# A hybrid encoder block on one core: the score matmul over the low rotary keys with 128 rows in place of 64

## The chip, the core and the metric

The kernel runs on one core of a Trainium2 chip. A core has five engines that run their own instruction streams and meet through semaphores: PE (the matrix engine, with its weight loads shown as PEld), DVE (vector), ACT (scalar), POOL and SP, which here only starts transfers. The metric is the device time of one execution in microseconds (us), as the median of several runs. Times inside an execution come from one execution that the hardware profiler recorded.

## What is computed

One layer of an encoder block is applied to two batches of 512 tokens, each of width 1024, in float32. The input is normalised and projected; a convolution branch and an attention branch follow, are gated, summed and projected again. The change lies in the attention branch, cut here to what matters:

```python
q = rms_norm(q, q_head_g)            # 8 heads, 128 plain + 64 rotary columns
k = rms_norm(k, k_head_g)            # the 64 rotary columns are shared by the heads
q = concat([q[..., :128], apply_rope(q[..., 128:], cos, sin)])
k = concat([k[..., :128], apply_rope(k[..., 128:], cos, sin)])
s = einsum('bqhd,bkhd->bhqk', q, k) / sqrt(192)
o = einsum('bhqk,bkhd->bqhd', softmax(s), v)
```

## The kernel before

PE works on operands in a 32-bit form of reduced precision (float32r). To keep the accuracy, each float32 operand is split into a high part, rounded to that form, and a low part, the difference; a product is the sum of high by high, high by low and low by high. So one logical matmul is several instructions that accumulate in one PSUM bank.

The program has stages: the input projection and the convolution branch (to about 640 us), the latent projections (to about 740 us), the attention (to about 1030 us), and two dense blocks, the output projection of the attention (L228) and the last projection (L864). The stage of interest is the attention. It runs over 16 units, a unit being one head and one batch, and in each unit over four blocks of 128 queries, so there are 64 blocks.

`stage_a` (L524 on) prepares a unit in four pieces, run one unit ahead: keys and values (L540 to L542, banks pkv), queries (L568 to L570, bank pq), and the transposed operands of the scores. The rotary keys are scaled on POOL (`krs`, L561). The tile `kk` holds them in three slots of 64 columns: slots 0 and 1 get the rounded high part twice from ACT (L562), slot 2 gets the low part from POOL (L563), which subtracts the high part from `krs`. PE transposes the two high slots together (L600, four instructions of 128 by 128) and the low slot (L602, four of 128 rows by 64 columns); ACT copies the results to SBUF as `k1` (L604, 128 rows: the high part twice, one under the other) and `k2` (L605, 64 rows: the low part). The rotary queries `qrT` hold the high part in rows 0 to 63 and the low part in rows 64 to 127.

`scores` (L608 on) makes one block: five matmuls of 512 columns into one bank `sc`, L612 to L614 for the 128 plain dimensions, L615 with all 128 rows of `qrT` against `k1` (high by high plus low by high in one instruction), and L616 with rows 0 to 63 of `qrT` against `k2` (high by low). Then DVE takes the row maximum (L619, L620), ACT the exponential with its sum (L622), DVE divides (L623, L624). Two blocks later `transp` (L631) transposes the probabilities on PE, ACT and DVE split them (L632, L633), and `av` (L641 to L643) multiplies by the values.

The order in which the engines get their instructions is not written out by hand in this stage: the code is a loop over blocks, and a scheduler in the tile framework, which runs the program on its own timing model, places the instructions of each engine. A change in an instruction's size can therefore move others. In each engine's queue instructions run in that order. All tiles of eight PSUM banks come from one pool (`bank`).

Of the kernel before, what the change touches and what calls it, by code (L numbers as in the profile page):

```python
# [10 lines left out]
F32R = mybir.dt.float32r  # L11
# [6 lines left out]
P = 128  # L18
D = 1024
S = 512  # L20
# [3 lines left out]
RD = 64  # L24
# [19 lines left out]
def encoder_block(tc, xp_d, xs_d, win_d, wkr_d, whd_d, wqr_d, wo_d, wp_d, wout_d, vec_d, dwk_d, rg_d, rc_d, yp_d, ys_d):  # L44
    nc = tc.nc
    opened = {}

    def open_pool(name, **kw):
        if kw.get("space") is not DRAM:
            kw["reuse_waits"] = "tile"  # L50
        cm = tc.tile_pool(name=name, **kw)
        opened[name] = cm
        return cm.__enter__()
# [5 lines left out]
    f = lambda ap: ap.bitcast(F32)  # L59
    mm = nc.tensor.matmul  # L60
# [7 lines left out]
    def bc(ap, n):  # L68
        return ap.unsqueeze(2).to_broadcast([ap.shape[0], ap.shape[1], n])
# [17 lines left out]
    identr = cp.tile([P, P], F32R, name="identr")  # L87
# [89 lines left out]
    def rsqrt(out, v):  # L177
        nc.gpsimd.tensor_tensor(out, v, mhalf[:, : v.shape[1]], op=ALU.pow)
# [57 lines left out]
    def block(i, xh=hh, xl=hl, ahead=2):  # L236
        ps = fresh(i)
        block_mm(ps, i, xh, xl, (0, 1))
        prep(i + ahead)
        return flat(ps)  # L240
# [77 lines left out]
    for j in range(KD):  # L318
        ps = flat(first[0]) if j == 0 else block(J["cb", j])
# [3 lines left out]
        ps = flat(first[1]) if j == 0 else block(J["ca", j])  # L323
        u = cv.tile([P, 2, UW], F32, tag="u", name=f"u{j}", bufs=4)
# [82 lines left out]
    for j in range(KD):  # L407
        ps = block(J["p", j], lambda k, b: cH[k][:, b * S : (b + 1) * S], lambda k, b: cL[k][:, b * S : (b + 1) * S])
# [8 lines left out]
    tx = open_pool("tx", bufs=2, side="left")  # L417
# [3 lines left out]
    def tmp(shape, name):  # L421
        return tx.tile(shape, F32, tag="tmp", name=name, bufs=4)
# [60 lines left out]
    qrT = {}  # L483
# [40 lines left out]
    def stage_a(h, b):  # L524
        whi, wlo = wdone[J["h", h]]
        qh_w, ql_w = (w[:, : 3 * P].rearrange("p (k c) -> p k c", k=3) for w in (whi, wlo))
        kh_w, kl_w = (w[:, 3 * P : 896].rearrange("p (k c) -> p k c", k=2) for w in (whi, wlo))
        u = f"{h}_{b}"
        s4 = slice(4 * b, 4 * b + 4)
        r = {}  # L530
        two = lambda tag, shape=None, bufs=2: at.tile(shape or [P, S], F32R, tag=tag, name=f"{tag}{u}", bufs=bufs)

        pk = two_banks(f"pkv{u}", F32)
        for i, ps in enumerate(pk):
            for t2 in range(2):
                o = (2 * i + t2) * P
                for k in range(2):
                    kh_ = lat["kv", 0, k, b][:, o : o + P]
                    kl_ = lat["kv", 1, k, b][:, o : o + P]
                    mm(ps[:, t2], kh_, kh_w[:, k], start=(k == 0), stop=False)  # L540
                    mm(ps[:, t2], kh_, kl_w[:, k], start=False, stop=False)  # L541
                    mm(ps[:, t2], kl_, kh_w[:, k], start=False, stop=(k == 1))  # L542
        ksq_ = tmp([P, 4, P], f"ksq{u}")
        sk = tx.tile([P, 4], F32, tag="sk", name=f"sk{u}")
        rk = tx.tile([P, 4], F32, tag="rk", name=f"rk{u}")
        for i in range(2):
            ACT(ksq_[:, 2 * i : 2 * i + 2], pk[i][:, :, 0:P], AF.Square)
        DVE.reduce_sum(sk, ksq_, axis=AX.X)
        DVE.tensor_add(sk, sk, skr[:, s4])
        DVE.tensor_scalar(sk, sk, 1.0 / QKD, EPS, op0=ALU.mult, op1=ALU.add)  # L550
        rsqrt(rk, sk)
        vh, vl = two("vh", [P, 4, P], bufs=3), two("vl", [P, 4, P], bufs=3)
        for i in range(2):
            sl = slice(2 * i, 2 * i + 2)
            nc.scalar.copy(vh[:, sl], pk[i][:, :, P : 2 * P])
            DVE.tensor_sub(vl[:, sl], pk[i][:, :, P : 2 * P], f(vh[:, sl]))
        r["vh"], r["vl"] = vh, vl
        yield r
        krs = tx.tile([P, 4, RD], F32, tag="krs", name=f"krs{u}", bufs=1)
        kk = tx.tile([P, 4, 3, RD], F32R, tag="big", name=f"kk{u}")  # L560
        nc.gpsimd.tensor_mul(krs, kro[:, s4], bc(rk, RD))  # L561
        nc.scalar.copy(kk[:, :, 0:2], krs.unsqueeze(2).to_broadcast([P, 4, 2, RD]))  # L562
        nc.gpsimd.tensor_sub(kk[:, :, 2], krs, f(kk[:, :, 0]))  # L563

        ps = bank([P, S], F32, f"pq{u}")
        for k in range(3):
            xh_, xl_ = lat["cq", 0, k, b], lat["cq", 1, k, b]
            mm(ps, qh_w[:, k], xh_, start=(k == 0), stop=False)  # L568
            mm(ps, qh_w[:, k], xl_, start=False, stop=False)
            mm(ps, ql_w[:, k], xh_, start=False, stop=(k == 2))  # L570
        sqt = tmp([P, S], f"qsq{u}")
        ACT(sqt, ps, AF.Square)
        r["qh"], r["ql"] = two("qh"), two("ql")
        ACT(r["qh"], ps, AF.Identity, scale=gqk)
        DVE.scalar_tensor_tensor(r["ql"], ps, gqk, f(r["qh"]), op0=ALU.mult, op1=ALU.subtract)
        ks = tmp([P, 4, P], f"ks{u}")
        for t in range(4):
            ACT(ks[:, t], pk[t // 2][:, t % 2, 0:P], AF.Identity, scale=rk[:, t : t + 1])
        yield r
        pst = bank([P, 4], F32, f"pqs{u}")  # L580
        for t in range(4):
            mm(pst[:, t : t + 1], sqt[:, t * P : (t + 1) * P], ones[:, 0:1], start=True, stop=True)  # L582
        sv = tx.tile([P, 4], F32, tag="sv", name=f"sv{u}")
        DVE.tensor_add(sv, pst, ssr[:, s4, h])
        DVE.tensor_mul(sv, sv, rq2[:, s4])
        DVE.tensor_scalar_add(sv, sv, QKD * EPS)
        rsqrt(sv, sv)
        r["sq"] = sqs[h, b]
        DVE.tensor_mul(r["sq"], sv, rq[:, s4])

        pT = bank([P, S], F32, f"pkT{u}")
        for t in range(4):
            nc.tensor.transpose(pT[:, t * P : (t + 1) * P], ks[:, t], identf)
        r["kh"], r["kl"] = two("kh"), two("kl")
        nc.scalar.copy(r["kh"], pT)
        DVE.tensor_sub(r["kl"], pT, f(r["kh"]))
        pT1 = bank([P, S], F32R, f"pkr1{u}")
        pT2 = bank([RD, S], F32R, f"pkr2{u}")
        for t in range(4):
            nc.tensor.transpose(pT1[:, t * P : (t + 1) * P], kk[:, t, 0:2].rearrange("p a d -> p (a d)"), identr)  # L600
        for t in range(4):
            nc.tensor.transpose(pT2[:, t * P : (t + 1) * P], kk[:, t, 2], identr)  # L602
        r["k1"], r["k2"] = two("k1"), two("k2", [RD, S])
        nc.scalar.copy(r["k1"], f(pT1))  # L604
        nc.scalar.copy(r["k2"], f(pT2))  # L605
        yield r

    def scores(h, b, j, r):  # L608
        u = f"{h}_{b}_{j}"
        js = slice(j * P, (j + 1) * P)  # L610
        ps = bank([P, S], F32, f"sc{u}")
        mm(ps, r["qh"][:, js], r["kh"], start=True, stop=False)  # L612
        mm(ps, r["qh"][:, js], r["kl"], start=False, stop=False)  # L613
        mm(ps, r["ql"][:, js], r["kh"], start=False, stop=False)  # L614
        mm(ps, qrT[h, b][:, js], r["k1"], start=False, stop=False)  # L615
        mm(ps, qrT[h, b][0:RD, js], r["k2"], start=False, stop=True)  # L616
        nm = ap_.tile([P, 1], F32, tag="nm", name=f"nm{u}", bufs=4)
        sm = ap_.tile([P, 1], F32, tag="sm", name=f"sm{u}", bufs=4)
        DVE.reduce_max(nm, ps, axis=AX.X, negate=True)  # L619
        DVE.tensor_mul(nm, nm, r["sq"][:, j : j + 1])  # L620
        pr = ap_.tile([P, S], F32, tag="pr", name=f"pr{u}", bufs=3)
        ACT(pr, ps, AF.Exp, bias=nm, scale=r["sq"][:, j : j + 1], accum_out=sm)  # L622
        DVE.reciprocal(sm, sm)  # L623
        DVE.tensor_scalar_mul(pr, pr, sm)  # L624
        return pr
# [27 lines left out]
    bank = lambda shape, dt, name: p1.tile(shape, dt, tag="p1", name=name)  # L653

    def two_banks(name, dt):
        pair = pp.tile([P, 2, 2, 2 * P], dt, tag="pp", name=name)
        return [pair[:, i] for i in range(2)]
# [10 lines left out]
    with tc.manual_schedule(engines={nc.tensor.engine}):  # L668
# [8 lines left out]
        for b in range(2):  # L677
            ps = p1.tile([P, S], F32, tag="p1", name=f"rrow{b}")
# [42 lines left out]
    for b in range(2):  # L721
        s4 = slice(4 * b, 4 * b + 4)
        rope(pkr[:, s4], kro[:, s4], kt2[:, s4], rt[:, 2], rt[:, 3])
    ga = stage_a(*units[0])
    next(ga)
    next(ga)
# [15 lines left out]
    bank = lambda shape, dt, name: ps8.tile(shape, dt, tag="b", name=name)  # L742
# [19 lines left out]
    for s_ in range(4 * NU + 3):  # L762
        n, j = divmod(s_, 4)
        if n < NU:
            h, b = units[n]
# [61 lines left out]
    for j in range(KD):  # L827
        ps = block(J["o", j], lambda k, b: aH[k, b], lambda k, b: aL[k, b])
        a, c = gates[j]
# [24 lines left out]
    for t in range(8):  # L854
# [3 lines left out]
        for grp in ((0, 1),) if t < 7 else ((0,), (1,)):  # L858
            ps = pp.tile([P, 2, S], F32, tag="pp", name=f"po{t}_{grp[0]}")
# [82 lines left out]
```

## Time and profile before

| what | value |
|---|---|
| median of 3 runs | 1207.74 us (1207.09 to 1209.12) |
| the profiled execution | 1209.62 us, of it 1207.8 us span |
| PE busy | 1190.6 us, 99% of the span |
| PE weight loads | 983.6 us, 81% |
| DVE busy | 758.1 us, 63% |
| ACT busy | 399.7 us, 33% |
| POOL busy | 74.3 us, 6% |

The span runs from the first to the last instruction; the profiled execution's own time is a little longer. Busy shares are means over all stages. A matmul's duration in the trace covers its way through the array and overlaps the next one's, so what it costs PE is read from the distance between the starts of neighbours, not from its duration. A label such as 64\*128 on a PE row gives the rows and columns of the stationary block.

### The profile page before, as it was taken

The numbers are of one execution on the slowest core, as the hardware profiler recorded it, in microseconds if no ns is written. First come the engines' busy times: TensorE is split into PE (matmuls) and PEld (weight loads), VectorE is DVE, ScalarE is ACT, GpSimd is POOL, SyncE is SP. The second block draws the span as 40 slices with busy tenths as digits, with TensorE's granted clock in tenths as the row PEclk, the third lists the DMA queues.
The fourth block names the chain that finished last, engine by engine and source line by source line (L and its number), as shares of the span: only waits on it lengthen the run. The fifth ranks groups of instructions, "written<-read, shape, count | busy, mean of one in ns | idle before, by whom it ended". The sixth has DMA issues, their size and how long they took to land.

```text
span 1207.8 us, 14730 instructions
## 1 busy us (share of the span) xinstructions
PE 1190.6 (99%) x5988; PEld 983.6 (81%) x5988; DVE 758.1 (63%) x1094; ACT 399.7 (33%) x698; POOL 74.3 (6%) x108
## 2 busy tenths in 40 slices
PE   7999999999999999999999999999999999999998
PEld 5788888888888888888888887888888887888887
DVE  4599999999999853332222363777777788343411
ACT  5411221121212113341012345756676677111200
POOL 3000000000000000000000012111111121000000
PEclk9999999999999999999999999999999999999999
DMA  5122212222123321113431111100100012244531
GB/s 209 36 88 87 64 60 87 70 70 85 55 71 105 105 70 37 52 53 139 157 122 35 40 66 56 40 19 25 34 25 24 31 36 85 83 132 163 183 105 70
DMA packets 27571, 92.71 MB, mean 77 GB/s; under 512 B 3184, under 2 KB 3440, under 8 KB 27504
## 3 DMA queue, kind: packets, MB, share of 16 engines
q1 hardware_dynamic: 23760, 79.19, 19.2%
q10 hardware_dynamic: 3744, 12.58, 3.2%
q8 instruction: 47, 0.77, 0.2%
q14 instruction: 20, 0.16, 0.0%
HBM read 70.79 MB, written 20.97 MB: 76 GB/s over the span
## 4 chain that ended last, share of the span: by engine, by line
PE 97%; DVE 1%; ACT 1%; DMA 1%; issue 0%; SPq 0%; POOL 0%; DVEq 0%; ACTq 0%
PE blk L228 62%; PE po L864 7%; PE sc L616 2%; PE pt L631 2%; PE av L642 2%; PE pkv L540 1%; PE av L641 1%; PE pkv L542 1%; PE pkv L541 1%; PE sc L612 1%; PE sc L613 1%; PE sc L614 1%; PE sc L615 1%; PE av L643 1%; PE pqs L582 1%; PE pq L568 1%
## 5 line engine op out<-in xcount | busy, mean ns | idle before, releaser
L228 PE MATMUL blk<-hH,whi 128*128 128x512 f32 x848 | 332.4, 393 | 1.6 <-ACT hH L209 0.7
L228 PE MATMUL blk<-hL,whi 128*128 128x512 f32 x848 | 332.6, 392 | 0.2 <-DVE hL L210 0.2
L253 DVE SCALAR_TENSOR_TENSOR y<-u,dwk,y 128x1024 f32<-128x1024 f32 x240 | 298.6, 1283 | 5.1 <-ACT y L250 1.4
L124 ACT CAST whi<-raw 128x1024 fp32r<-128x1024 f32 (+2 forms) x81 | 83.7, 1033 | 557.4 <-PE blk L228 540.7
L228 PE MATMUL blk<-hH,wlo 128*128 128x512 f32 x848 | 265.3, 391 | 0.3 <-DVE rr L191 0.2
L228 PEld LDWEIGHTS blk<-hH,whi 128*128 128x128 f32 x848 | 160.0, 189 | 36.3 <-ACT hH L209 1.4
L228 PEld LDWEIGHTS blk<-hH,wlo 128*128 128x128 f32 x848 | 160.1, 189 | 34.0 <-DVE wlo L125 1.1
L228 PEld LDWEIGHTS blk<-hL,whi 128*128 128x128 f32 x848 | 160.0, 189 | 33.9 <-DVE hL L210 1.3
L125 DVE TENSOR_TENSOR wlo<-raw,whi 128x1024 fp32r<-128x1024 f32 (+1 forms) x80 | 96.4, 1205 | 128.0 <-ACT whi L124 128.0
L228 PE MATMUL blk<-a,whi 128*128 128x512 f32 x256 | 68.4, 389 | 0.0
L622 ACT ACTIVATE pr<-sc,nm,sqs 128x512 f32<-128x512 f32 x64 | 50.9, 795 | 22.7 <-DVE nm L620 22.6
L228 PEld LDWEIGHTS blk<-a,whi 128*128 128x128 f32 x256 | 48.0, 188 | 9.9
L619 DVE TENSOR_REDUCE nm<-sc 128x1 f32<-128x512 f32 x64 | 44.0, 687 | 13.6 <-PE sc L616 13.1
L410 DVE TENSOR_TENSOR tmc<-blk,smc 128x1024 f32<-128x1024 f32 x8 | 9.8, 1225 | 65.1 <-PE blk L228 65.1
L867 DVE TENSOR_TENSOR o<-po,xr 128x1024 f32<-128x1024 f32 (+1 forms) x9 | 10.0, 1107 | 64.3 <-PE po L864 64.3
L228 PE MATMUL blk<-cL,whi 128*128 128x512 f32 x128 | 49.8, 389 | 0.0
L228 PE MATMUL blk<-cH,whi 128*128 128x512 f32 x128 | 49.8, 390 | 0.0
L633 DVE TENSOR_TENSOR pt<-pt,pt 128x512 fp32r<-128x512 f32 x64 | 43.6, 683 | 1.2 <-ACT pt L632 0.7
L632 ACT CAST pt<-pt 128x512 fp32r<-128x512 f32 x64 | 38.4, 604 | 8.4 <-PE pt L631 8.2
L228 PE MATMUL blk<-a,wlo 128*128 128x512 f32 x128 | 39.4, 389 | 0.0
L228 PE MATMUL blk<-cH,wlo 128*128 128x512 f32 x128 | 39.4, 389 | 0.0
L642 PE MATMUL av<-pt,vh 128*128 128x256 f32 x128 | 38.6, 302 | 0.2 <-DVE pt L633 0.2
(203 smaller groups left out, 1856.2 us busy)
## 6 DMA issues: line engine op xcount, KB each, us to landing
raw<-in_win_dram SPq DMA_DIRECT2D x53, 512.0 KB, 3.6
mc_s<-stmc ACTq DMA_DIRECT2D x8, 512.0 KB, 2.9
ga_s<-stga ACTq DMA_DIRECT2D x8, 512.0 KB, 3.3
raw<-in_wp_dram SPq DMA_DIRECT2D x8, 512.0 KB, 5.0
smc<-mc_s SPq DMA_DIRECT2D x8, 512.0 KB, 4.6
tc_s<-tmc SPq DMA_DIRECT2D x8, 512.0 KB, 3.0
sga<-ga_s SPq DMA_DIRECT2D x16, 256.0 KB, 2.6
raw<-in_wo_dram SPq DMA_DIRECT2D x8, 512.0 KB, 4.3
```

Of the source, the lines that this page charges most:

```text
L124: nc.scalar.copy(hv, rv)
L125: DVE.tensor_sub(lv, rv, f(hv))
L228: mm(ps[:, b], (wlo if wl_ else whi)[:, k], xl(k, b) if xl_ else xh(k, b), start=(k == 0 and wl_ == 0 and xl_ == 0), stop=(k == KD - 1 and ...
L253: DVE.scalar_tensor_tensor(yt, u[:, :, i : i + S], dwk[:, j, i : i + 1], yt, op0=ALU.mult, op1=ALU.add)
L616: mm(ps, qrT[h, b][0:RD, js], r["k2"], start=False, stop=True)
L619: DVE.reduce_max(nm, ps, axis=AX.X, negate=True)
L622: ACT(pr, ps, AF.Exp, bias=nm, scale=r["sq"][:, j : j + 1], accum_out=sm)
L631: nc.tensor.transpose(pt[:, kt], pr[:, kt * P : (kt + 1) * P], identf)
L632: nc.scalar.copy(pth[:, :, js], pt)
L633: DVE.tensor_sub(ptl[:, :, js], pt, f(pth[:, :, js]))
L642: mm(ps, r["vh"][:, kt], ptl[:, kt], start=False, stop=False)
L864: mm(ps[:, n], lhs[k][:, ts_], w[k][:, n * S : (n + 1) * S], start=first_, stop=last_)
```

## The change

The low rotary keys are stored twice, one copy under the other, and the last score matmul uses all 128 rows of `qrT` in place of its upper 64. It then adds, beside high by low, the product of low by low as well. For that `kk` gets a fourth slot, the subtraction on POOL writes slots 2 and 3 at once, the transposes of L602 take two slots (128 columns in place of 64), the bank `pkr2` and the tile `k2` have 128 partitions in place of 64, and so has the ACT copy between them. No tile moves to another place in SBUF. A line is added, so lines from 563 on have one number more in the changed program.

```diff
-        kk = tx.tile([P, 4, 3, RD], F32R, tag="big", name=f"kk{u}")
+        kk = tx.tile([P, 4, 4, RD], F32R, tag="big", name=f"kk{u}")
         nc.gpsimd.tensor_mul(krs, kro[:, s4], bc(rk, RD))
         nc.scalar.copy(kk[:, :, 0:2], krs.unsqueeze(2).to_broadcast([P, 4, 2, RD]))
-        nc.gpsimd.tensor_sub(kk[:, :, 2], krs, f(kk[:, :, 0]))
+        both = lambda a: a.unsqueeze(2).to_broadcast([P, 4, 2, RD])
+        nc.gpsimd.tensor_sub(kk[:, :, 2:4], both(krs), f(kk[:, :, 0:2]))
...
-        pT2 = bank([RD, S], F32R, f"pkr2{u}")
+        pT2 = bank([P, S], F32R, f"pkr2{u}")
...
-            nc.tensor.transpose(pT2[:, t * P : (t + 1) * P], kk[:, t, 2], identr)
-        r["k1"], r["k2"] = two("k1"), two("k2", [RD, S])
+            nc.tensor.transpose(pT2[:, t * P : (t + 1) * P], kk[:, t, 2:4].rearrange("p a d -> p (a d)"), identr)
+        r["k1"], r["k2"] = two("k1"), two("k2")
...
-        mm(ps, qrT[h, b][0:RD, js], r["k2"], start=False, stop=True)
+        mm(ps, qrT[h, b][:, js], r["k2"], start=False, stop=True)
```

PE around the first score of the first unit. In a row, what is written stands ahead of the arrow and what is read behind it; `pkr_0_4860` is the bank of the low keys, `sc_0_0_4889` that of the scores. Before:

```order
L600 MATMUL pkr_0_4859<-identr,kk_0_4720 128x128 x4
L602 MATMUL pkr_0_4860<-identr,kk_0_4720 64x128 x4
L612 MATMUL sc_0_0_4889<-kh_0_4855,qh_0_4736 128x512
L613 MATMUL sc_0_0_4889<-kl_0_4856,qh_0_4736 128x512
L614 MATMUL sc_0_0_4889<-kh_0_4855,ql_0_4737 128x512
L615 MATMUL sc_0_0_4889<-k_0_4869,qrT_0_4751 128x512
L616 MATMUL sc_0_0_4889<-k_0_4870,qrT_0_4751 128x512
L540 MATMUL pkv_1_0_4903<-whi_4593,kvH_1_4260 128x256
```

and now:

```order
L601 MATMUL pkr_0_4859<-identr,kk_0_4720 128x128 x4
L603 MATMUL pkr_0_4860<-identr,kk_0_4720 128x128 x4
L613 MATMUL sc_0_0_4889<-kh_0_4855,qh_0_4736 128x512
L614 MATMUL sc_0_0_4889<-kl_0_4856,qh_0_4736 128x512
L615 MATMUL sc_0_0_4889<-kh_0_4855,ql_0_4737 128x512
L616 MATMUL sc_0_0_4889<-k_0_4869,qrT_0_4751 128x512
L617 MATMUL sc_0_0_4889<-k_0_4870,qrT_0_4751 128x512
L540 MATMUL pkv_1_0_4903<-whi_4593,kvH_1_4260 128x256
```

Nothing moved here: only the output of the four transposes has 128 partitions in place of 64. The rows of the last score matmul read alike, since the sizes shown are those of its output; its two operands have 128 partitions in place of 64.

PE at the first score of the second unit of the first head, beside the query matmuls (`pq`) of the next unit. Before:

```order
L614 MATMUL sc_1_0_5132<-kh_1_5032,ql_1_4962 128x512
L615 MATMUL sc_1_0_5132<-k_1_5046,qrT_1_4990 128x512
L568 MATMUL pq_0_5151<-cqH_0_4279,whi_4829 128x512
L569 MATMUL pq_0_5151<-cqL_0_4280,whi_4829 128x512
L616 MATMUL sc_1_0_5132<-k_1_5047,qrT_1_4990 128x512
L570 MATMUL pq_0_5151<-cqH_0_4279,wlo_4830 128x512
```

and now:

```order
L615 MATMUL sc_1_0_5132<-kh_1_5032,ql_1_4962 128x512
L616 MATMUL sc_1_0_5132<-k_1_5046,qrT_1_4990 128x512
L617 MATMUL sc_1_0_5132<-k_1_5047,qrT_1_4990 128x512
L569 MATMUL pq_0_5151<-cqH_0_4279,whi_4829 128x512
L570 MATMUL pq_0_5151<-cqL_0_4280,whi_4829 128x512
L571 MATMUL pq_0_5151<-cqH_0_4279,wlo_4830 128x512
```

The last score matmul moved two places ahead, to directly behind the one that uses the same stationary block.

ACT in the unit of head 1 and the second batch, where the rotary keys are copied (`k_1_5501` is the high part, `k_1_5502` the low one) between the exponentials (`pr`) of the unit before. Before:

```order
L595 CAST kh_1_5487<-pkT_1_5482 128x512
L604 CAST k_1_5501<-pkr_1_5491 128x512
L605 CAST k_1_5502<-pkr_1_5492 64x512
L622 ACTIVATE pr_0_2_5467,sm_0_2_5464<-sc_0_2_5457,nm_0_2_5463,sqs_0_4044 128x512
L632 CAST pt_5519<-pt_0_0_5521 128x4x128
```

and now:

```order
L596 CAST kh_1_5487<-pkT_1_5482 128x512
L605 CAST k_1_5501<-pkr_1_5491 128x512
L623 ACTIVATE pr_0_2_5467,sm_0_2_5464<-sc_0_2_5457,nm_0_2_5463,sqs_0_4044 128x512
L606 CAST k_1_5502<-pkr_1_5492 128x512
L633 CAST pt_5519<-pt_0_0_5521 128x4x128
```

The copy of the low keys went behind an exponential; the matmul that reads it belongs to the next unit's first score.

## Rows read from the trace of the kernel before

**Rows 1.** The page, its part on the chain that ended last: shares by engine.
```profile
PE 97%; DVE 1%; ACT 1%; DMA 1%; issue 0%; SPq 0%; POOL 0%; DVEq 0%; ACTq 0%
```

**Rows 2.** PE's waits, 735 to 1030 us: us in total, times, longest us.
```profile
PE pkr L602 <- ACT k L604: 1.9, 1, 1.9
PE av L641 <- ACT pt L632: 0.7, 1, 0.7
```

**Rows 3.** Windows: length; busy us of PE, PEld, DVE, ACT, POOL; clock, DMA share, GB/s.
```profile
740.00:1025.00 285.00, 284.78 (x1847) 234.26 (x1847) 214.64 (x559) 193.40 (x459) 53.49 (x60) 1.00 0.11 37
...
992.00:1010.00 18.00, 18.00 (x118) 14.63 (x117) 16.18 (x42) 14.94 (x34) 4.40 (x4) 1.00 0.13 46
```

**Rows 4.** PE's timeline, two scores and transposes: start us, duration us, instruction.
```profile
780.69 0.40 PE L613 MATMUL sc<-kl,qh 128*128 128x512 f32 x1
780.92 0.40 PE L614 MATMUL sc<-kh,ql 128*128 128x512 f32 x1
781.16 0.39 PE L615 MATMUL sc<-k,qrT 128*128 128x512 f32 x1
781.48 0.49 PE L616 MATMUL sc<-k,qrT 64*128 64x512 f32 x1
781.90 0.39 PE L642 MATMUL av<-pt,vh 128*128 128x256 f32 x1
782.12 0.28 PE L643 MATMUL av<-pt,vl 128*128 128x256 f32 x1
782.24 0.28 PE L641 MATMUL av<-pt,vh 128*128 128x256 f32 x1
...
784.45 0.39 PE L615 MATMUL sc<-k,qrT 128*128 128x512 f32 x1
784.76 0.49 PE L616 MATMUL sc<-k,qrT 64*128 64x512 f32 x1
785.18 1.05 PE L582 MATMUL pqs<-ones,qsq 128*128 128x1 f32 x8
...
786.49 0.54 PE L600 MATMUL pkr<-identr,kk 128*128 128x128 f32 x4
786.86 0.41 PE L602 MATMUL pkr<-identr,kk 128*64 128x128 f32 x4
787.11 0.34 PE L641 MATMUL av<-pt,vh 128*128 128x256 f32 x1
```

**Rows 5.** The weight loads' timeline at the first of these scores, with idle time.
```profile
781.48 0.18 PEld L616 LDWEIGHTS sc<-k,qrT 64*128 64x128 f32 x1 [0.36 <-issue]
781.90 0.19 PEld L642 LDWEIGHTS av<-pt,vh 128*128 128x128 f32 x1 [0.24 <-issue]
```

**Rows 6.** ACT groups, 740 to 1025 us, by form: busy us, mean ns | idle.
```profile
L604 ACT CAST k<-pkr 128x512 fp32r<-128x512 f32 x16 | 9.6, 601 | 0.0
L605 ACT CAST k<-pkr 64x512 fp32r<-64x512 f32 x16 | 9.3, 583 | 0.9 <-PE pkr L602 0.9
```

**Rows 7.** PE's timeline in the rotary key projection, at 689 us.
```profile
689.31 0.40 PE L695 MATMUL blk<-hL,whi 128*64 128x512 f32 x1
689.55 0.39 PE L698 MATMUL blk<-hH,whi 128*128 128x512 f32 x1
```

**Rows 8.** Timelines of POOL and PE: low keys and their transposes, units 1 and 15.
```profile
751.65 0.73 POOL L563 TENSOR_TENSOR kk<-krs,kk 128x256 fp32r<-128x256 f32 x1 [2.19 <-ACT kk L562]
752.44 0.44 PE L602 MATMUL pkr<-identr,kk 128*64 128x128 f32 x4
...
1008.65 0.73 POOL L563 TENSOR_TENSOR kk<-krs,kk 128x256 fp32r<-128x256 f32 x1 [1.70 <-ACT kk L562]
1009.84 0.41 PE L602 MATMUL pkr<-identr,kk 128*64 128x128 f32 x4
```

**Rows 9.** Windows ahead of the attention, columns as in rows 3.
```profile
720.00:724.00 4.00, 3.54 (x27) 2.95 (x25) 2.98 (x10) 2.56 (x9) 1.46 (x2) 1.00 0.11 43
...
725.40:728.80 3.40, 3.40 (x10) 2.62 (x9) 0.86 (x2) 1.90 (x6) 1.30 (x2) 0.50 0.22 78
```

## The prediction

> **What bounds the kernel now.** I read the chain of work that ended last first: 97% of it is PE [rows 1], so time is lost or won where PE spends it. The table of PE's waits says the same from the other side: between 740 and 1030 us, the attention stage that holds all 64 scores, PE waits for another engine only twice that matter, 1.9 us at the start and 0.7 us at the end [rows 2]. The windows show who comes next: over 740 to 1025 us DVE is busy 214.64 of 285 us and ACT 193.40, but in the last stretch, 992 to 1010 us, DVE has 16.18 of 18 us [rows 3]. After that PE runs two blocks of plain matmuls, so what the attention stage saves moves the end by as much.
>
> Inside the stage I read PE's timeline by starts, not by durations: durations overlap, while the distance from one start to the next is what a matmul takes from the engine. One score is five matmuls of 512 columns, L612 to L616. The ordinary distance is 0.23 or 0.24 us (780.69 to 780.92 to 781.16). Around the 64-row one it is not: L615 to L616 takes 0.32 us, L616 to the next matmul 0.42, and that next matmul, of 256 columns, 0.22 where the one behind it takes 0.12 [rows 4]. The timeline of weight loads shows why: the load of L616 starts at 781.48, the moment its matmul starts, after 0.36 us of idle time put down to issue, and the load after it also starts only with its own matmul, after 0.24 us idle [rows 5]. So the 64-row load and the one behind it are not done ahead, under the matmul before, as the other loads are.
>
> The Trainium skill has two rules on this. Its page "TensorEngine Tiling (Array Packing)", section Tiling Modes, says that a change of tiling mode drains the engine. By that rule the 64-row matmul costs two drains and a 128-row one none, and rows 4 agree. It goes too far for columns, as the 64-column matmuls show next.
>
> A narrower form is no slower everywhere: the matmul of L695, 128 rows by 64 columns, stands between 128 by 128 ones at an ordinary distance, 689.31 to 689.55 [rows 7]. What costs here goes with the 64 rows, and this matters for the transposes, whose form also changes.
>
> **The change part by part.**
>
> *The score matmul (L616, 64 of them).* It becomes a 128-row matmul of the same 512 columns with the same stationary block that L615 has just used. I take it to go like L612 to L615. With a matmul of 256 columns behind it, the three distances from L615 on sum to 781.16 to 782.12, 0.96 us; ordinary ones would be 0.24 + 0.23 + 0.12 = 0.59. That leaves 0.37 us. With the one-column matmuls of L582 behind it, 784.45 to 785.18 is 0.73 against 0.24 + 0.23 = 0.47; of the eight short ones themselves I count nothing: 0.26 us [rows 4]. In the order of the changed program 45 of the 64 have a matmul of 256 or 512 columns behind them and 19 have a short one. 45 x 0.37 + 19 x 0.26 = 16.7 + 4.9 = 21.6 us. The bounds: 64 x 0.26 = 16.6 and 64 x 0.39 = 25.0, the latter if each of the three distances is 0.01 longer than the rounding shows. I take 21.6, since both kinds are read off directly.
>
> *The transposes (L602, 16 groups of four).* The stationary block gets 128 columns in place of 64. Four of 64 columns take from 786.86 to 787.11, 0.25 us; the four of L600 just ahead, 128 columns, take 786.49 to 786.86, 0.37 us [rows 4]. So 0.12 x 16 = 1.9 us more on PE, all of it on the path. Bounds 1.0 and 2.5.
>
> *The ACT copy of the result (L605).* It has the same 512 elements in each partition, on 128 partitions in place of 64: 583 ns against 601 for the same copy at L604 [rows 6]. That is 16 x 0.02 = 0.3 us on ACT, which is no bound: nothing. In several units the scheduler puts this copy behind an exponential (shown with the change), which costs its reader some 0.8 us; its first reader comes with the next unit's first score, usually microseconds later, so I cost it at nothing; if the cover were gone it would be 0.8 us a unit, and it counts into the second rival.
>
> *The subtraction on POOL (L563).* It makes 512 elements in each partition in place of 256, at 0.73 us now. No row shows the larger one. It lies between no longer at all and twice as long, +0.73; a row of 256 elements that costs little more than a fixed part cannot be told from one that costs by the element, so I take +0.6, close to the upper end. What hides it is the time until PE reaches L602. In unit 1 POOL ends at 751.65 + 0.73 = 752.38 and PE's L602 starts at 752.44: 0.06 us of cover. In the last unit it is 1009.38 and 1009.84: 0.46 [rows 8]. PE also comes earlier, by two scores between the unit's query matmuls and its L602, 2 x 0.37 = 0.74 us. So PE will wait 0.6 + 0.74 - 0.06 = 1.3 us in unit 1 and 0.6 + 0.74 - 0.46 = 0.9 in the last: 2.2 us. In the other units I expect the kk chain to be done earlier. Queued behind a waiting L602 on PE are the transposes of probabilities and the next value matmuls. The power step on POOL behind the subtraction also starts up to 0.6 us later; its result scales the next unit's scores, which are well behind it: nothing.
>
> *The end of the attention stage.* The window 992 to 1010 us holds four scores; without 4 x 0.37 = 1.5 us it is 16.5 us long, with 16.18 us of DVE work in it [rows 3]. There, and in the last unit, DVE sets the pace. The last two units hold nine or so scores whose 0.37 us make 3.3 us; I count half of that as lost, 1.5 us (bounds 0 and 3.3). Elsewhere DVE goes from 214.64 of 285 to the same of about 265, 81%, still behind PE.
>
> *The order.* Only a few PE rows move: some 64-row matmuls now stand directly behind L615, one group of key and value matmuls goes ahead of value products. No work is added by that. No DMA is added or moved.
>
> The sum: 21.6 - 1.9 - 2.2 - 1.5 = 16.0 us saved. The profiled execution took 1209.62 us, 1207.8 of span and 1.8 around it, so it would be 1193.6; it lies 1.9 us above the median of the timed runs, 1207.74, and against that median the forecast is 1191.7 us. With the bounds: 25.0 - 1.0 - 1.0 - 0 = 23 at best, though then DVE has to follow everywhere, and 16.6 - 2.5 - 3.5 - 3.3 = 7.3 at worst. I take 1186.5 to 1198.5 for this case.
>
> **The rivals.**
>
> *PE meets the vector side in every unit.* If all sixteen units lost at L602 what the last one loses, 16 x 0.9 = 14.4 us in place of 2.2, there would be 21.6 - 1.9 - 14.4 - 1.5 = 3.8 us left, 1203.9 us; between that and the forecast everything is possible. For it speaks that DVE rises to 81% and the longer POOL step; against it, that of PE's waits in the stage only those of rows 2 have any size, one at its start and one at its end.
>
> *The surplus stays.* The long distances could belong not to the 64 rows but to the second use of the same stationary block or to the last matmul of an accumulation. Then the change saves nothing and adds the transposes and the POOL waits: 1207.7 + 1.9 to 1207.7 + 1.9 + 2.2, 1209.6 to 1211.8 us. Against it: L613 uses the stationary block of L612 again and goes at an ordinary distance into L614, 780.69 to 780.92 [rows 4]. A rule of the Trainium skill would give this rival: "TensorE: Matmul & The Clock Gate", section Why this matters for your kernels, has it that a single matmul of few rows takes as long as one of 128. Rows 4 speak against it, since the 64-row one takes longer.
>
> *PE's clock falls (the slower side).* In the 720 to 724 us stretch PE was busy 3.54 of 4 us with transposes and one-column matmuls and short waits, and from 725.40 to 728.80 the granted clock was 0.50, the level of 1.2 GHz [rows 9]. In those 3.4 us half of the work, 1.7 us, is lost. New waits at L602 stand in the same mix of one-column matmuls and transposes. If that brought a fall in each of 16 units, 16 x 1.7 = 27 us would be lost, and the kernel would be 1207.7 + 27 - 16 = 1218.7 us; it decides from ten falls on, 17 us. Against it: the granted clock is 1.00 over the whole stage, 740 to 1025 us, right after a wait of 1.9 us [rows 2, 3].
>
> **How the numbers follow.** Forecast 0.84, the vector side 0.10, the surplus that stays 0.04, the clock 0.02. A measurement of this kernel can tell 0.2%, 2.4 us. Forecast and first rival are faster: 0.94. The second is split, 0.02 within and 0.02 slower, the third is slower: 0.02 and 0.04. The forecast's own span holds 0.84, so the range is 1186.5 to 1198.5.
>
> **What would show it.** In the profile after: the distances L615 to its successor, from there to the next, and of the next matmul itself should be 0.24, 0.23 and 0.12; weight loads of that line should have no issue idle time. Four L602 transposes should take 0.37 us. L563's mean should be 1.2 to 1.5 us, and PE's waits should have rows for L602 on POOL with about 2 us in total, and more than before at the end of the stage. The two blocks behind should keep their length. The prediction is wrong if the loads still come late, if waits of PE on ACT, DVE or POOL sum to over 8 us in the stage, or if the granted clock falls in it.

## The result and the profile after

The changed kernel takes 1191.05 us (1187.43 to 1191.45, 4 runs), the kernel before on the same chip 1207.82 us (4 runs). The ratio is 0.9852, with a 95% interval of 0.9836 to 0.9867: 16.8 us less, where 16.0 were forecast. The profiled execution took 1190.66 us, of it 1188.9 us span, against 1209.62 and 1207.8 before. L616 of before is L617 here, L602 is L603 and L563 is L564.

PE's timeline first, at the same two scores as rows 4. Columns: start us, duration us, instruction.

```profile
780.26 0.40 PE L616 MATMUL sc<-k,qrT 128*128 128x512 f32 x1
780.49 0.39 PE L617 MATMUL sc<-k,qrT 128*128 128x512 f32 x1
780.72 0.28 PE L643 MATMUL av<-pt,vh 128*128 128x256 f32 x1
780.84 0.28 PE L644 MATMUL av<-pt,vl 128*128 128x256 f32 x1
...
783.17 0.40 PE L616 MATMUL sc<-k,qrT 128*128 128x512 f32 x1
783.41 0.39 PE L617 MATMUL sc<-k,qrT 128*128 128x512 f32 x1
783.63 0.95 PE L583 MATMUL pqs<-ones,qsq 128*128 128x1 f32 x8
...
784.83 0.54 PE L601 MATMUL pkr<-identr,kk 128*128 128x128 f32 x4
785.21 0.51 PE L603 MATMUL pkr<-identr,kk 128*128 128x128 f32 x4
785.55 0.35 PE L642 MATMUL av<-pt,vh 128*128 128x256 f32 x1
```

The three distances behind L616 are 0.23, 0.23 and 0.12 us, where rows 4 have 0.32, 0.42 and 0.22. The weight loads of the same place, which answer to rows 5, show it from the other side:

```profile
780.26 0.19 PEld L617 LDWEIGHTS sc<-k,qrT 128*128 128x128 f32 x1
780.50 0.19 PEld L643 LDWEIGHTS av<-pt,vh 128*128 128x128 f32 x1
```

Each load now starts 0.2 us ahead of its matmul, under the one before, and the idle time put down to issue is gone. It is gone at every score. Of the weight loads' waits over 735 to 1030 us, before, the largest row is this one (us in total, times, longest); the same view now has no row for L617:

```profile
PEld sc L616 <- issue: 21.3, 59, 0.4
```

PE's waits, 735 to 1030 us, as rows 2: us in total, times, longest.

```profile
PE pkr L603 <- ACT k L605: 1.9, 1, 1.9
PE pkr L603 <- POOL kk L564: 1.7, 3, 0.8
PE av L642 <- ACT pt L633: 0.7, 1, 0.7
PE sc L613 <- ACT pr L623: 0.3, 1, 0.3
PE pkr L601 <- ACT kk L562: 0.2, 1, 0.2
```

The second row is new and costs most. PE's timeline at two of its three places (the third is unit 14), units 1 and 15, with the wait in brackets, and POOL's ahead of the first:

```profile
749.96 0.63 PE L594 MATMUL pkT<-identf,ks 128*128 128x128 f32 x4
750.82 0.53 PE L601 MATMUL pkr<-identr,kk 128*128 128x128 f32 x4 [0.23 <-ACT kk L562]
752.17 0.75 PE L603 MATMUL pkr<-identr,kk 128*128 128x128 f32 x4 [0.82 <-POOL kk L564]
...
992.57 0.53 PE L603 MATMUL pkr<-identr,kk 128*128 128x128 f32 x4 [0.63 <-POOL kk L564]
```

```profile
750.84 1.27 POOL L564 TENSOR_TENSOR kk<-krs,kk 128x512 fp32r<-128x512 f32 x1 [2.17 <-ACT kk L562]
```

In unit 1 of the kernel before, PE's rows ahead of the L602 of rows 8 were:

```profile
751.52 0.63 PE L593 MATMUL pkT<-identf,ks 128*128 128x128 f32 x4
751.91 0.54 PE L600 MATMUL pkr<-identr,kk 128*128 128x128 f32 x4
```

POOL's step takes 1.27 us in place of 0.73. The windows, columns as in rows 3: the whole stage from the first score to the first matmul of the output projection, a stretch behind the wait of unit 1, and one near the end.

```profile
739.98:1010.94 270.96, 267.73 (x1877) 246.36 (x1877) 218.59 (x565) 195.50 (x461) 62.03 (x60) 0.99 0.12 40
...
752.06:755.47 3.41, 3.30 (x13) 2.92 (x14) 3.26 (x8) 3.41 (x7) 1.48 (x2) 0.50 0.00 0
972.00:990.00 18.00, 17.37 (x118) 15.59 (x117) 16.36 (x41) 15.20 (x36) 4.81 (x4) 1.00 0.10 27
```

The stage is 270.96 us long. Before it ran from 740.40 to 1029.90, 289.50 us:

```profile
740.40:1029.90 289.50, 288.63 (x1878) 237.88 (x1877) 218.11 (x565) 195.54 (x461) 53.49 (x60) 1.00 0.11 37
```

Behind the new wait the granted clock was 0.50 for 3.41 us, which in the profile of before happened only ahead of the stage [rows 9]. The stage fixes the rest: what follows it has the same length to 0.1 us.

### The profile page after: what moved, and what is told of

It reads as the page before. It is cut to its first block, busy times and chain, and to the rows that moved or that the text cites. A ratio compares the mean times of both kernels' runs of the same rounds, so it can differ in the third digit from the quotient of the medians.

```text
span 1188.9 us, 14723 instructions
## 1 busy us (share of the span) xinstructions
PE 1169.9 (98%) x5988; PEld 992.2 (83%) x5988; DVE 758.9 (64%) x1094; ACT 399.6 (34%) x698; POOL 83.4 (7%) x108
## 4 chain that ended last, share of the span: by engine, by line
PE 94%; ACT 2%; DVE 1%; DMA 1%; POOL 1%; issue 0%; SPq 0%; ACTq 0%; DVEq 0%
PE blk L228 63%; PE po L865 7%; PE pt L632 2%; PE pkv L540 1%; PE pkv L542 1%; PE pkv L541 1%; PE av L642 1%; PE av L643 1%; PE av L644 1%; PE sc L613 1%; PE sc L615 1%; PE sc L614 1%; PE sc L616 1%; PE sc L617 1%; PE pq L569 1%; PE pq L570 1%
## 5 line engine op out<-in xcount | busy, mean ns | idle before, releaser
L228 PE MATMUL blk<-hH,whi 128*128 128x512 f32 x848 | 332.5, 393 | 1.6 <-ACT hH L209 0.7
L228 PE MATMUL blk<-hL,whi 128*128 128x512 f32 x848 | 332.6, 392 | 0.2 <-DVE hL L210 0.2
L228 PE MATMUL blk<-hH,wlo 128*128 128x512 f32 x848 | 265.2, 391 | 0.3 <-DVE wlo L125 0.2
L228 PEld LDWEIGHTS blk<-hH,whi 128*128 128x128 f32 x848 | 160.0, 189 | 36.4 <-ACT hH L209 1.4
L228 PEld LDWEIGHTS blk<-hH,wlo 128*128 128x128 f32 x848 | 160.0, 189 | 34.1 <-DVE wlo L125 1.1
L228 PEld LDWEIGHTS blk<-hL,whi 128*128 128x128 f32 x848 | 160.1, 189 | 33.9 <-DVE hL L210 1.3
L228 PE MATMUL blk<-a,whi 128*128 128x512 f32 x256 | 68.4, 389 | 0.0
L228 PEld LDWEIGHTS blk<-a,whi 128*128 128x128 f32 x256 | 48.0, 188 | 9.9
L228 PE MATMUL blk<-cL,whi 128*128 128x512 f32 x128 | 49.8, 389 | 0.0
L228 PE MATMUL blk<-cH,whi 128*128 128x512 f32 x128 | 49.8, 390 | 0.0
L228 PE MATMUL blk<-a,wlo 128*128 128x512 f32 x128 | 39.4, 389 | 0.0
L228 PE MATMUL blk<-cH,wlo 128*128 128x512 f32 x128 | 39.4, 389 | 0.0
L632 PE MATMUL pt<-identf,pr 128*128 128x128 f32 x256 | 38.9, 275 | 0.0
```

The costliest lines, as they stand in the source:

```text
L228: mm(ps[:, b], (wlo if wl_ else whi)[:, k], xl(k, b) if xl_ else xh(k, b), start=(k == 0 and wl_ == 0 and xl_ == 0), stop=(k == KD - 1 and ...
L632: nc.tensor.transpose(pt[:, kt], pr[:, kt * P : (kt + 1) * P], identf)
```

## The experiments

Theory: at the 64-row matmul PE changes between 128 and 64 rows and back, and at each change a weight load can't be done ahead. Rivals: the surplus belongs to the second use of a stationary block or to closing the bank; or the gain came with the new order; and on the cost side, POOL is hidden anyway. Stage lengths below are read as for the kernel after, from the start of the first score to the first L228 with the attention's output. They leave out what differs earlier: the first score starts at 736.3 to 738.4 us in the four experiments that pad the tile with zeros (e1, e2, e7, e8) and at 739.2 to 741.9 in the others, and that is in the medians. This difference is there by PE's 41st matmul, at 17.2 to 17.9 us against 19.4 to 20.7, long before any instruction that was changed, so it isn't taken for a gain of the edits. The runs e5_64_first, e7_96_rows and e8_wide_transposes are from another chip, where the kernel before took 1208.93 us in place of 1207.76; each ratio is against the kernel before on the same chip.

**e1_score_only.** The tile of the low keys is allocated once per batch, its lower half is set to zero, and only the score matmul gets 128 rows. The order on PE, ACT and DVE is that of before.

```diff
-        r["k1"], r["k2"] = two("k1"), two("k2", [RD, S])
+        r["k1"] = two("k1")
+        if h == 0:
+            k2t[b] = two("k2")
+            nc.gpsimd.memset(f(k2t[b][RD:P]), 0.0)
+        r["k2"] = k2t[b]
...
-        nc.scalar.copy(r["k2"], f(pT2))
+        nc.scalar.copy(r["k2"][0:RD], f(pT2))
...
-        mm(ps, qrT[h, b][0:RD, js], r["k2"], start=False, stop=True)
+        mm(ps, qrT[h, b][:, js], r["k2"], start=False, stop=True)
```

> Only the score matmul gets 128 rows: the low keys lie in the upper 64 rows of a tile whose lower 64 rows are zero, written once. POOL, the transposes and the ACT copy keep the sizes of before, and so does the order on PE. Theory (the 64-row matmul keeps its own weight load and the next one from being done ahead): the three distances at each score become ordinary, 22 to 24 us less on PE, of which about 1 us is lost to POOL in the second unit and 1 to 2 at the end: 1185 to 1189 us, below the changed kernel's 1191. Rival (the surplus stays with the last matmul of the bank, and the gain came with the new order): 1205 us or more.

Measured: 1183.45 us (4 runs), ratio 0.9795 (0.9778 to 0.9813): 24.3 us less than before, and more than the change itself brought. It beats both kernels, and the intervals of its ratio and the changed kernel's do not overlap. Of the 7.6 us between these two, 4.6 lie in the stage by the profiles and 2.4 ahead of it. The window of its stage:

```profile
737.58:1003.92 266.34, 264.47 (x1879) 243.34 (x1877) 214.66 (x565) 193.90 (x461) 54.21 (x60) 1.00 0.13 40
```

289.50 - 266.34 = 23.2 us came out of the stage. PE's busy time in it fell by 288.63 - 264.47 = 24.2 us, and 1.0 us of that went into new waits, 0.3 of it for POOL. With the order of before and its preparation untouched, the whole gain of the stage lies in the number of rows of 64 matmuls. The expectation's lower end, 1185, was still too high.

**e2_pool_long.** As e1_score_only, but POOL writes two copies.

```diff
-        kk = tx.tile([P, 4, 3, RD], F32R, tag="big", name=f"kk{u}")
+        kk = tx.tile([P, 4, 4, RD], F32R, tag="big", name=f"kk{u}")
...
-        nc.gpsimd.tensor_sub(kk[:, :, 2], krs, f(kk[:, :, 0]))
+        both = lambda a: a.unsqueeze(2).to_broadcast([P, 4, 2, RD])
+        nc.gpsimd.tensor_sub(kk[:, :, 2:4], both(krs), f(kk[:, :, 0:2]))
```

> As e1_score_only, but POOL writes the low keys twice as in the change (512 elements, 1.28 us in place of 0.73); the transposes still read one copy. Theory: PE waits for POOL in the second unit and in the last three, 1.5 to 2 us, and a fall of the granted clock behind the first wait costs up to 2 more: 1188 to 1190 us, that is 1.5 to 4 over e1_score_only. Rival (POOL is hidden): within 0.7 us of e1_score_only.

Measured: 1186.46 us (4 runs), ratio 0.9815 (0.9798 to 0.9832), 3.0 us over e1_score_only. This kernel, like e1_score_only, was expected at least 1.5 us slower than it is; the difference between the two is as expected, between 1.5 and 4. Its windows (the stage; a stretch behind the wait of unit 1) and its wait, then that of e1_score_only:

```profile
738.23:1007.50 269.27, 266.00 (x1878) 244.64 (x1877) 217.86 (x565) 194.89 (x461) 62.80 (x60) 0.99 0.12 40
...
750.30:753.70 3.40, 3.27 (x13) 2.89 (x14) 3.27 (x8) 3.37 (x8) 1.49 (x2) 0.50 0.00 0
```

```profile
PE pkr L605 <- POOL kk L566: 1.8, 3, 0.8
```

```profile
PE pkr L604 <- POOL kk L565: 0.3, 1, 0.3
```

The stage is 2.93 us longer than in e1_score_only. Length less PE's busy time is 3.27 us against 1.87: 1.4 more of waiting, all of it for POOL. PE's busy time is 266.00 against 264.47: 1.5 more, with the same work, in the stretch at half the granted clock. So POOL isn't hidden, and in this execution its waits cost twice. The fall of the clock doesn't always come: one execution had a mean granted clock of 1.000 and took 1184.19 us, 0.9 to 1.8 over the two of e1_score_only with that clock. The order on the engines is that of the changed kernel, not that of e1_score_only; the two parts, 1.4 and 1.5, leave nothing for it.

**e8_wide_transposes.** As e1_score_only, but the low keys come first in `kk`, the high copies move to slots 1 and 2, and the transposes of the low keys take a high copy along.

```diff
-        nc.gpsimd.tensor_sub(kk[:, :, 2], krs, f(kk[:, :, 0]))
+        nc.gpsimd.tensor_sub(kk[:, :, 0], krs, f(kk[:, :, 1]))
...
-            nc.tensor.transpose(pT2[:, t * P : (t + 1) * P], kk[:, t, 2], identr)
+            nc.tensor.transpose(pT2[:, t * P : (t + 1) * P], kk[:, t, 0:2].rearrange("p a d -> p (a d)"), identr)
```

> As e1_score_only, but the transposes of the low keys take 128 columns (the low keys and a high copy beside them, which is not used further); POOL writes 256 elements. It shows the transposes' cost by itself: 16 x 0.10 to 0.12 = 1.6 to 1.9 us over e1_score_only's 1183.5, so 1184.5 to 1186.5 us.

Measured: 1185.84 us (4 runs), ratio 0.9811 (0.9796 to 0.9825). The transposes of the low keys on PE's timeline:

```profile
781.68 0.51 PE L604 MATMUL pkr<-identr,kk 128*128 128x128 f32 x4
782.02 0.35 PE L647 MATMUL av<-pt,vh 128*128 128x256 f32 x1
```

Four take 0.34 us, where rows 4 have 0.25: 0.09 x 16 = 1.4 us. The stage, 738.42 to 1006.28, is 267.86 us, 1.5 over e1_score_only. The medians, from two chips, differ by 2.4, with spreads of 3 to 4 us each; the stage tells it closer.

**e3_prep_only.** The change with its score matmul put back.

```diff
-        mm(ps, qrT[h, b][:, js], r["k2"], start=False, stop=True)
+        mm(ps, qrT[h, b][0:RD, js], r["k2"][0:RD], start=False, stop=True)
```

> All of the preparation of the change (POOL, transposes, copy of 128 rows), but the score matmul reads 64 rows as before. Theory: the costs of the change without its gain, 1.5 us of transposes and 0.6 to 2 us of POOL: 1209 to 1212 us. Rival (the gain comes with the new order or the tile of 128 rows): 1204 us or less.

Measured: 1212.36 us (10 runs), ratio 1.0031 (1.0019 to 1.0044), just above the expected range. The new order brings no gain by itself; the whole is 4.6 us slower than before. Its waits for POOL are small, since PE comes later:

```profile
PE pkr L603 <- POOL kk L564: 0.5, 1, 0.5
```

The profiled execution, 1213.79 us, had two stretches of 3.4 us at a granted clock of 0.50 inside the stage:

```profile
740.20:743.60 3.40, 3.40 (x14) 2.80 (x14) 1.40 (x4) 1.97 (x3) 0.00 (x0) 0.50 0.26 103
753.80:757.20 3.40, 3.40 (x10) 2.12 (x9) 3.13 (x9) 2.75 (x6) 1.14 (x1) 0.50 0.00 0
```

The stage, 739.21 to 1034.08, is 294.87 us, 5.4 over that of before. By the rows the two stretches lose 3.4 us, half of 6.8; with 1.4 to 1.5 for the transposes and 0.5 for the wait that accounts for it. The first stretch is no cost of the preparation: in the profiles of before and after, one such stretch lies ahead of the stage.

**e4_64_twice.** The kernel before, its 64-row matmul issued twice.

```diff
-        mm(ps, qrT[h, b][0:RD, js], r["k2"], start=False, stop=True)
+        mm(ps, qrT[h, b][0:RD, js], r["k2"], start=False, stop=False)
+        mm(ps, qrT[h, b][0:RD, js], r["k2"], start=False, stop=True)
```

> The kernel before with its 64-row score matmul issued twice in a row, so each score adds the low key product once more. If the surplus comes with a change between 128 and 64 rows, the second one costs an ordinary 0.23 us: 64 x 0.23 = 14.7, 1221 to 1224 us. If each 64-row matmul has it, the second one costs 0.42 us: 27 us, 1233 to 1236 us.

Measured: 1223.47 us (4 runs), ratio 1.0126 (1.0110 to 1.0143): 15.7 us for 64 matmuls, 0.245 us each. PE's timeline, then the weight loads of the same place:

```profile
784.98 0.39 PE L615 MATMUL sc<-k,qrT 128*128 128x512 f32 x1
785.30 0.50 PE L616 MATMUL sc<-k,qrT 64*128 64x512 f32 x1
785.63 0.39 PE L617 MATMUL sc<-k,qrT 64*128 64x512 f32 x1
785.96 0.39 PE L643 MATMUL av<-pt,vh 128*128 128x256 f32 x1
786.18 0.28 PE L644 MATMUL av<-pt,vl 128*128 128x256 f32 x1
```

```profile
785.29 0.18 PEld L616 LDWEIGHTS sc<-k,qrT 64*128 64x128 f32 x1 [0.36 <-issue]
785.40 0.19 PEld L617 LDWEIGHTS sc<-k,qrT 64*128 64x128 f32 x1
785.96 0.19 PEld L643 LDWEIGHTS av<-pt,vh 128*128 128x128 f32 x1 [0.37 <-DVE wlo L125]
```

The distances are 0.32, 0.33, 0.33 and 0.22, against ordinary 0.24, 0.23, 0.23 and 0.12: 0.38 us of surplus, as much as with a single 64-row matmul. The load of the second one starts 0.23 us ahead of its matmul, like any other; the first one's and the one behind the pair start only with theirs. The surplus comes with going in and out, not with each 64-row matmul. The 0.42 us behind the single one can then be read as 0.23 with 0.1 of the way in and 0.1 of the way out.

The profiled execution, 1226.11 us, lies above the median: at the start of its stage the granted clock was 0.50 for 6.8 us, though this kernel prepares its keys as before. Less the 3.4 us lost there, the stage (739.29 to 1046.39) gives 0.22 us for each added matmul.

```profile
740.40:747.20 6.80, 6.80 (x28) 6.10 (x28) 1.93 (x5) 2.63 (x6) 0.00 (x0) 0.50 0.13 51
```

**e5_64_first.** The 64-row matmul as the first of the five.

```diff
-        mm(ps, r["qh"][:, js], r["kh"], start=True, stop=False)
+        mm(ps, qrT[h, b][0:RD, js], r["k2"], start=True, stop=False)
+        mm(ps, r["qh"][:, js], r["kh"], start=False, stop=False)
...
-        mm(ps, qrT[h, b][:, js], r["k1"], start=False, stop=False)
-        mm(ps, qrT[h, b][0:RD, js], r["k2"], start=False, stop=True)
+        mm(ps, qrT[h, b][:, js], r["k1"], start=False, stop=True)
```

> The kernel before, with the 64-row matmul as the first of the five of a score in place of the last. The matmul behind it is now the first high by high one, with another stationary block, and it no longer closes the bank. Theory (the surplus belongs to the change between 128 and 64 rows): two changes a score remain, 64 x 0.37 = 24 us of surplus in place of 23.5, so 1206 to 1210 us. Rival (the surplus comes from using one stationary block twice in a row, or from closing the bank): it goes, 1184 to 1190 us.

Measured: 1210.69 us (10 runs), ratio 1.0009 (1.0000 to 1.0019), 0.7 us above the expected range. PE has a new wait of 0.7 us for the copy of the low keys, which the first matmul of the first score now needs. PE's timeline:

```profile
783.37 0.50 PE L612 MATMUL sc<-k,qrT 64*128 64x512 f32 x1
783.80 0.50 PE L613 MATMUL sc<-kh,qh 128*128 128x512 f32 x1
784.14 0.40 PE L614 MATMUL sc<-kl,qh 128*128 128x512 f32 x1
784.37 0.39 PE L615 MATMUL sc<-kh,ql 128*128 128x512 f32 x1
784.60 0.40 PE L616 MATMUL sc<-k,qrT 128*128 128x512 f32 x1
784.83 0.28 PE L642 MATMUL av<-pt,vh 128*128 128x256 f32 x1
```

The surplus went along: 0.43 and 0.34 us behind the 64-row matmul, while the one that now closes the bank goes at 0.23. Neither the shared stationary block nor the end of the bank causes it.

**e7_96_rows.** As e1_score_only, with 96 rows.

```diff
-        mm(ps, qrT[h, b][:, js], r["k2"], start=False, stop=True)
+        mm(ps, qrT[h, b][0:96, js], r["k2"][0:96], start=False, stop=True)
```

> As e1_score_only, but the score matmul reads 96 rows in place of 128 (the low keys in 64, zeros in 32). The array is then not divided, though a quarter of its rows is idle. If the surplus comes with dividing the array into halves of 64 rows, it is gone: within 1.5 us of e1_score_only's 1183.5. If it comes with any number of rows but 128, it is there as before: 1205 to 1209 us.

Measured: 1183.94 us (4 runs), ratio 0.9796 (0.9780 to 0.9813), as e1_score_only. PE's timeline:

```profile
774.43 0.40 PE L621 MATMUL sc<-k,qrT 128*128 128x512 f32 x1
774.67 0.39 PE L622 MATMUL sc<-k,qrT 96*128 96x512 f32 x1
774.90 0.28 PE L648 MATMUL av<-pt,vh 128*128 128x256 f32 x1
775.02 0.28 PE L649 MATMUL av<-pt,vl 128*128 128x256 f32 x1
```

A matmul of 96 rows goes at ordinary distances. So it isn't "fewer than 128" that costs. In the program the 64-row matmul addresses the array as a part of 64 by 128, the 96-row one the whole of it; the surplus goes with the part. Whether 64 rows that address the whole would be free of it, no run shows.

## Why the prediction was right

**The mechanism** was right: two weight loads at each 64-row matmul not done ahead, gone with 128 rows. The Trainium skill's page "TensorEngine Tiling (Array Packing)", section Tiling Modes, says that a change of tiling mode drains the engine, and rows 4, e4_64_twice and e5_64_first agree that a change between 128 and 64 rows has a price, 0.38 us for going in and out; for columns it says more than the runs show, since matmuls of 128 rows by 64 columns go without surplus [rows 7]. The rule of the Trainium skill's page "TensorE: Matmul & The Clock Gate", section Why this matters for your kernels, that a single matmul of few rows takes as long as one of 128 holds for the 96-row matmul and, by the total, for the second of two 64-row ones (0.245 us), not at a change.

**The main term was too small.** The forecast was 21.6 us. For the 19 scores with a short matmul behind them I counted nothing in what follows. From 784.45 to L600 at 786.49 rows 4 have 2.04 us; the same stretch now takes from 783.17 to 784.83, 1.66 us. It is 0.38 there too: the way out also delays the eight one-column matmuls. 64 x 0.38 = 24.3 us, inside the bounds given, at their upper part. e1_score_only agrees: PE's busy time in the stage fell by 24.2 us.

**The transposes** were forecast at 1.9 us. They cost 0.34 against 0.25 us in four, 16 x 0.09 = 1.4, and 1.5 by e8_wide_transposes.

**POOL**: the step got 0.54 us longer, 0.6 was taken. PE waits for it in unit 1 and at the end, as forecast. The waits listed sum to 1.7 us in place of 2.2, but they count from the modelled end of the row ahead; the starts say more. In unit 1, from L594 to L603 takes 752.17 - 749.96 = 2.21 us, where from L593 to L602 took 0.92: 1.29 more, as forecast (1.3), a part of it ahead of L601, which waits for the high copies. In unit 15, from L601 to L603 takes 1.17 us where 0.37 is ordinary: 0.8 more, forecast 0.9. Units 13 and 14, which were taken to be covered, have 0.46 and 0.81, another 0.5. That is 2.6 us in all. One reading was wrong: the 0.06 us in unit 1 were no cover. From L600 to L602 took 0.53 us there, so PE already stood 0.16 us, and the changed kernel has the same 0.06 us between POOL's end, 750.84 + 1.27 = 752.11, and PE's start.

**The end of the stage** was forecast to lose 1.5 us to DVE. That step failed: DVE rose to 16.36 of 18 us, but PE's longest wait there is 0.7 us as before [rows 2], and only one of 0.3 us, on ACT, was added. A share of 90% near the bound didn't mean a loss.

**The clock** was a rival at 0.02, as a fall in every unit. One fall came, in one unit, behind the wait for POOL. It isn't in the sum, and by the prediction's own last sign any fall in the stage speaks against it, so here it failed. In 3.41 us at half the level 1.7 us are lost by the rows; e2_pool_long shows 1.5. The fall doesn't come in every execution: the three executions of the changed kernel with a mean clock of 0.997 took 1190.7 to 1191.5 us, the one with 0.999 took 1187.4.

The sum in the profiled execution: 24.3 - 1.4 - 2.6 - 0.3 - 1.7 = 18.3, and the stage got 18.5 us shorter; the spans differ by 18.9, since the first score also came 0.4 us earlier. In the medians it is 16.8, since the profiled execution before lay 1.9 us above its median and the one after 0.4 below. So the forecast of 16.0 was close by chance: the gross term was 2.7 too small, the transposes 0.5 and the end 1.2 too dear, POOL 0.4 too cheap, some 4 us of gain missed on balance. The missing fall of the clock, 1.7 us, and the 2 us between profiled executions and medians took it back. The parts also add up across the experiments: e1_score_only's stage of 266.34, plus 2.93 for POOL, plus 1.5 for the transposes, is 270.8 against the changed kernel's 270.96.

That the wait for POOL brings the fall of the clock is argued from the order of events, not tested by itself. For it: the three profiles with such a wait of 0.5 us or more in unit 1 (the changed kernel, e2_pool_long, e3_prep_only) have a fall there. Against it: the execution of e2_pool_long without a fall, and the falls at the start of the stage in e3_prep_only, e4_64_twice and e5_64_first, behind a wait of 1.9 us that every profile has. What decides it stays open, and so does why the executions differ by up to 5.6 us ahead of the first score; that doesn't touch the stage.

## What to carry to other kernels

Read a matmul's cost from the distances of three starts, its own, the one ahead and the one behind: the 64-row matmul showed 0.49 us of duration and cost 0.38 us beyond an ordinary one, half of it at its neighbours. A single matmul on half of the rows amid 128-row ones is better padded with zero rows than left short, and padding with zeros that are written once costs less than a second copy made every time (here 266.34 us for the stage against 270.96); the second copy adds the product of low by low, the zeros don't. If PE is the bound, look at how little time lies between a helper engine's result and PE before lengthening that step: here PE already stood waiting in unit 1, and in the profiled executions the price was paid twice, in waits and in the clock.

## What was not expected of the hardware

A 96-row matmul has no surplus at all (1183.94 against 1183.45 us), a 64-row one 0.38 us, and two 64-row ones in a row the same 0.38 us together. A wait of 0.82 us on PE, amid transposes and one-column matmuls, was followed by 3.41 us at half the granted clock, while the wait of 1.9 us ahead of the first score was not in the profiles of before and after [rows 2, 3], but was in e3_prep_only, e4_64_twice (6.8 us) and e5_64_first. The length of a wait alone does not tell whether the clock falls.
